# The first row slice of the modulation taken in two halves, with the first half's loads issued ahead

## The chip, the core and the metric

The kernel runs on one core of a Trainium2 chip. Five engines work from queues of their own, each in program order: TensorE (PE; its weight loads are shown apart as PEld), VectorE (DVE), ScalarE (ACT), GpSimd (POOL) and SyncE (SP), which here only issues the loads and stores (its DMA queue is SPq). They wait for each other through semaphores. The metric is the device time of one execution in microseconds (us); lower is better.

## The reference, cut to what matters

One layer of a hybrid block on 256 latent and 256 context tokens of width 2048, all in float32. Only the start of it is touched by the change: a modulation vector made from a conditioning vector, an RMSNorm scaled and shifted by it, and a projection of the result.

```python
sh_m, sc_m, ... = split(silu(c) @ w_ada + b_ada, 6)        # latent tokens
csh_m, csc_m, ... = split(silu(c_ctx) @ w_ada + b_ada, 6)  # context tokens
hc = rmsnorm(ctx, norm_mix_w) * (1 + csc_m) + csh_m
hl = rmsnorm(x, norm_mix_w) * (1 + sc_m) + sh_m
p = hl @ w_in          # w_in: 2048 x 13376, columns x | B | C | dt | z | pool | fourier | gates
# SSD, pooling and Fourier branches of p, gated sum, w_out, gated residual,
# then RMSNorm, SwiGLU (w_ffn_gate, w_ffn_up, w_ffn_down), gated residual, final RMSNorm
```

## The kernel before

**Stages.** All large products run as a list of stages. A stage has one weight load of 512 KB (256 rows of a weight as a tile `raw` of 128 x 2 x 512) and matmuls that use it. Each float32 weight is split in two parts by `split` (lines 123 to 125): ACT casts it to fp32r (`whi`, line 124), then DVE subtracts to get the rest (`wlo`, line 125). `mm3` (lines 130 to 133) makes one product from three matmuls of 128x512: hi by hi, hi by lo, lo by hi. `stream` walks through the list: for stage i it first issues loads up to stage i + lead + 4 (`load_upto`), then writes the splits of all stages up to i + lead (`split_upto`), then the stage's own matmuls. `lead` is 2. So the cast of a later stage's weight stands in ACT's queue, and its subtraction in DVE's queue, ahead of the work of the stage that is being written.

**The first sixteen stages.** The 2048 rows of the input are cut into eight slices j of 256 rows, that is two row tiles k of 128. For slice j, two stages run: `stage_b` multiplies the slice by 512 columns of `w_in` into four PSUM accumulators `b_acc`, kept over all slices; `stage_x0` multiplies it by another 512 columns, into PSUM tiles `aux` that are copied or added to `x_sum` in SBUF (line 391 on ACT for j = 0, line 394 on DVE after that). At its end it adds the slice to `dt_acc` with weights `dtp` (lines 400 and 401), which are split from the load `dtw` by `split_dt`; that is written after stage 0. There are four PSUM banks for `aux` tiles; `dt_acc` holds one for all of these stages.

**The modulation of a slice.** Before slice j can be multiplied, its rows of `xnT` (the normalised tokens, turned by PE's transposes of line 285) are modulated. Shift and scale come from 4 MB of `w_ada`, eight loads of 512 KB (`fetch`). `ada_tile` multiplies each by `stat` (line 314: matmuls with 32 columns of weights, four side by side); after the eighth, ACT copies the sums to SBUF (`adasb`, line 318) and `ada_sums` adds them up over partitions (line 324). `modulate` makes scale and shift on DVE (lines 335 to 337), applies them (line 344), casts the result on ACT (`hh`, line 345) and subtracts on DVE (`hl`, line 348). For slices 1 to 7 these pieces stand between the matmuls of the slice before. For slice 0 nothing stands beside them: all of slice 0's eight loads, matmuls and steps are written ahead of the first stage.

**Queues.** All loads go through SP's one queue in the order in which they are written: constants, the eight token tiles, slice 0's eight `w_ada` loads, three `w_in` loads (`load_upto(3)`), slice 1's eight `w_ada` loads, `dtw`, then the rest from `stream`. ACT, DVE and PE run what is written for them in that order and let nothing pass.

Of the kernel before, what the change touches and what calls it, by code (L numbers as in the profile page):

```python
# [11 lines left out]
F32 = mybir.dt.float32  # L12
# [4 lines left out]
P = 128  # L17
# [65 lines left out]
def hybrid_block(ctx: ExitStack, tc, io):  # L83
# [20 lines left out]
    def load(dst, src):  # L104
        nc.sync.dma_start(dst, src)
# [4 lines left out]
    def Q(shape, dt=F32, nme="q"):  # L110
        return qp.tile(shape, dt, tag="Q", name=nm(nme))
# [15 lines left out]
    def rows(w, k0, nk, c0, n):  # L127
        return w[k0 * P : (k0 + nk) * P, c0 : c0 + n].rearrange("(k p) n -> p k n", p=P)
# [191 lines left out]
    def ada_sums(j):  # L320
        if j >= 8:
            return
        for i in range(4):
            T.matmul(aps[j][:, 2 * i : 2 * i + 2], aps[j, "sb"][:, i * P : (i + 1) * P], SEL, start=True, stop=True)

    def modulate(j):
        if j >= 8:
            return
        k2 = slice(2 * j, 2 * j + 2)

        def col(o):
            return pp[:, o + 2 * j : o + 2 * j + 2].unsqueeze(2).to_broadcast([P, 2, 2])

        r = aps[j][:, 0:8].rearrange("p (a b) -> p a b", b=2)
        V.tensor_tensor(Sm[:, k2, :], r[:, 0:2], col(PP_BSHM), ALU.add)
        V.tensor_tensor(Am[:, k2, :], r[:, 2:4], col(PP_BSCM), ALU.add)
        V.scalar_tensor_tensor(Am[:, k2, :], Am[:, k2, :], 1.0, col(PP_NM), ALU.add, ALU.mult)
        hh[j] = H([P, 2, CH], F32R, nme="hh")
        hl[j] = H([P, 2, CH], F32R, nme="hl")
        for k in range(2):  # L340
            kt = 2 * j + k
            for s in range(2):
                v = xnT[j][:, k, s * 256 : (s + 1) * 256]
                V.tensor_scalar(v, v, Am[:, kt, s : s + 1], Sm[:, kt, s : s + 1], ALU.mult, ALU.add)
            S.copy(hh[j][:, k, :], xnT[j][:, k, :])
            yield
        for k in range(2):
            V.tensor_tensor(hl[j][:, k, :], xnT[j][:, k, :], hh[j][:, k, :].bitcast(F32), ALU.subtract)

    for i in range(8):  # L350
        fetch(0, i)
    scale_rows(0)
    for t in range(1, 4):
        scale_rows(t)
# [7 lines left out]
    dtp = []  # L362
    dt_acc = []

    def feature(ps, parts, j, o, first, last):

        hi, lo = parts
        for k in range(2):
            mm3(ps, hi[:, k, o : o + P], lo[:, k, o : o + P], hh[j][:, k, :], hl[j][:, k, :],
                first and k == 0, last and k == 1)  # L370

    def stage_b(j):
        def mm(parts):
            for ct in range(4):
                feature(b_acc[ct], parts, j, ct * P, j == 0, j == 7)
                for i in (2 * ct, 2 * ct + 1):
                    ada_tile(j + 1, i)
                    fetch(j + 2, i)
        return mm

    def stage_x0(j):
        def mm(parts):
            mod = modulate(j + 1)
            for ct in range(4):
                if ct:
# [3 lines left out]
                if j == 0:
                    x_sum[0, ct] = Q([P, 2, 256], nme="xin")  # L390
                    S.copy(x_sum[0, ct].rearrange("p a b -> p (a b)"), ps)
                else:
                    v = x_sum[0, ct].rearrange("p a b -> p (a b)")
                    V.tensor_tensor(v, v, ps, ALU.add)
                if ct == 0:
                    ada_sums(j + 1)
            for k in range(2):
                kt = 2 * j + k
                w = dtp[kt // 8][:, kt % 8, :]
                T.matmul(dt_acc[0], w, hh[j][:, k, :], start=kt == 0, stop=False)  # L400
                T.matmul(dt_acc[0], w, hl[j][:, k, :], start=False, stop=kt == KT - 1)
        return mm

    for j in range(8):
        add(rows(w_in, 2 * j, 2, B_OFF, CH), CH, stage_b(j), room=0)
        add(rows(w_in, 2 * j, 2, 0, CH), CH, stage_x0(j), room=0)

    b_acc.extend(acc() for _ in range(4))
    dt_acc.append(aux())
    load_upto(3)  # L410
    for i in range(8):
        fetch(1, i)
    dtw = H([P, KT, 64], nme="dtw")
    load(dtw, rows(w_in, 0, KT, DT_OFF, 64))
    for i in range(8):
        ada_tile(0, i)
    ada_sums(0)

    dtp.extend(H([P, 8, P], F32R, nme="dtp") for _ in range(2))
    for _ in modulate(0):  # L420
        pass

    def split_dt():
        for i in range(2):
            split(dtp[i][:, :, 0:64], dtp[i][:, :, 64:128], dtw[:, 8 * i : 8 * i + 8, :])
    stages[0].after.append(split_dt)

    bin_ = []

# [1053 lines left out]
    plan_ada(u_all[:32], s_u, s_q)  # L1483
    plan_ada(u_all[32:], s_q, s_o + 10)
    plan_ada(units_of(G_F), s_g + 2, s_d - 4)
    load_upto(6)
    split_upto(1)
    stream()
    for e in list(beside):
# [80 lines left out]
```

## Time and profile before

| | |
|---|---|
| median of three runs | 1902.11 us (1901.12 to 1902.36) |
| the profiled execution's own time | 1902.28 us |
| its span on the core | 1900.5 us |
| PE busy | 1845.0 us (97%) |
| DVE busy | 1247.2 us (66%) |
| ACT busy | 855.0 us (45%) |
| chain that ended last: PE, DMA, DVE, ACT | 81%, 7%, 5%, 4% |
| mean granted TensorE clock | 0.992 |

The span is the time from the first to the last record of the core; 1.8 us of the execution's own time lie around it. The page of the profile also cuts the span into 40 slices of 47.5 us and gives each engine's busy share in them. The chain that ended last is followed back from the last instruction: at each step to what released it, or to the instruction before it on its engine.

### The profile page before, as it was taken

To read this page: it belongs to the slowest core of one execution; us is meant where nothing else is said; L and a number is where in the kernel's file an instruction comes from. 1 tells how busy PE (TensorE), PEld (TensorE's weight loads), DVE (VectorE), ACT (ScalarE), POOL (GpSimd) and SP (SyncE) were. 2 spreads that over 40 slices of the span, in tenths; PEclk is the share of its full clock that TensorE was granted. 3 is DMA by queue.
4 is the path that set the end of the run, shared out by engine and by line. 5 is a ranking of instruction groups with operands and counts; after the bars stand their busy time and mean duration, and the time that the engine had idled before them with its cause. 6 is when DMAs were issued, how large, how long until landed. Compare 5 with 4: busy or idle time off the path is not lost.

```text
span 1900.5 us, 23216 instructions
## 1 busy us (share of the span) xinstructions
PE 1845.0 (97%) x8796; PEld 1483.7 (78%) x8796; DVE 1247.2 (66%) x1508; ACT 855.0 (45%) x1216; POOL 0.2 (0%) x4
## 2 busy tenths in 40 slices
PE   5999999999999999999999998999999999999997
PEld 3667887777777788887777777888888888888885
DVE  4445785778777587777888654777655555555567
ACT  4323445637456474533434346444443444434434
POOL 0000000000000000000000000000000000000000
PEclk9999999999999999999999999999999999999998
DMA  9992332556657456789989754888756666556653
GB/s 330 358 342 75 114 112 67 179 169 216 201 163 242 142 178 211 220 256 321 332 315 322 267 199 129 284 282 288 257 190 196 190 188 188 190 197 189 191 192 127
DMA packets 211904, 409.19 MB, mean 215 GB/s; under 512 B 14672, under 2 KB 47568, under 8 KB 211792
## 3 DMA queue, kind: packets, MB, share of 16 engines
q1 hardware_dynamic: 211792, 407.71, 67.1%
q8 instruction: 69, 1.13, 0.3%
q14 instruction: 43, 0.35, 0.1%
HBM read 405.56 MB, written 2.10 MB: 215 GB/s over the span
## 4 chain that ended last, share of the span: by engine, by line
PE 81%; DMA 7%; DVE 5%; ACT 4%; issue 2%; SPq 1%; DVEq 0%; ACTq 0%
PE acc L131 23%; PE acc L133 23%; PE acc L132 23%; DMA raw<-w_ssd_out 4%; ACT whi L124 2%; PE aux L314 2%; DVE wlo L125 1%; DMA raw<-w_in 1%; DVE adacc L461 1%; DMA raw<-w_out 1%; PE aux L131 1%; PE aux L132 1%; PE aux L133 1%; PE aux L683 1%; PE aux L759 1%
## 5 line engine op out<-in xcount | busy, mean ns | idle before, releaser
L125 DVE TENSOR_TENSOR wlo<-raw,whi 128x1024 fp32r<-128x1024 f32 x548 | 669.4, 1223 | 564.9 <-ACT whi L124 559.9
L124 ACT CAST whi<-raw 128x1024 fp32r<-128x1024 f32 x548 | 575.3, 1052 | 805.0 <-PE acc L133 613.5
L131 PE MATMUL acc<-whi,h2h 128*128 128x512 f32 x700 | 273.6, 391 | 4.4 <-ACT h2h L124 4.4
L133 PE MATMUL acc<-whi,h2l 128*128 128x512 f32 x700 | 273.1, 390 | 0.0
L132 PE MATMUL acc<-wlo,h2h 128*128 128x512 f32 x700 | 272.6, 389 | 0.0
L131 PE MATMUL acc<-whi,lh 128*128 128x512 f32 x640 | 256.7, 401 | 3.5 <-ACT gt L981 3.3
L132 PE MATMUL acc<-wlo,lh 128*128 128x512 f32 x640 | 250.5, 391 | 2.4 <-DVE wlo L125 2.4
L133 PE MATMUL acc<-whi,ll 128*128 128x512 f32 x640 | 249.7, 390 | 0.0
L131 PEld LDWEIGHTS acc<-whi,h2h 128*128 128x128 f32 x700 | 131.5, 188 | 31.8 <-ACT h2h L124 5.0
L461 DVE SCALAR_TENSOR_TENSOR adacc<-araw,sil,adacc 128x1024 f32<-128x1024 f32 x120 | 153.4, 1278 | 2.1 <-DMA araw<-w_ada 2.0
L133 PEld LDWEIGHTS acc<-whi,h2l 128*128 128x128 f32 x700 | 131.5, 188 | 28.3 <-DVE h2l L125 0.9
L132 PEld LDWEIGHTS acc<-wlo,h2h 128*128 128x128 f32 x700 | 131.6, 188 | 27.1
L132 PEld LDWEIGHTS acc<-wlo,lh 128*128 128x128 f32 x640 | 120.3, 188 | 31.5 <-DVE wlo L125 5.6
L131 PEld LDWEIGHTS acc<-whi,lh 128*128 128x128 f32 x640 | 120.2, 188 | 31.5 <-ACT gt L981 4.1
L133 PEld LDWEIGHTS acc<-whi,ll 128*128 128x128 f32 x640 | 120.1, 188 | 25.3
L131 PE MATMUL acc<-whi,ah 128*128 128x512 f32 x336 | 131.0, 390 | 0.0
L133 PE MATMUL acc<-whi,al 128*128 128x512 f32 x336 | 130.7, 389 | 0.0
L132 PE MATMUL acc<-wlo,ah 128*128 128x512 f32 x336 | 130.7, 389 | 0.0
L131 PE MATMUL acc<-hh,whi 128*128 128x512 f32 x256 | 104.9, 410 | 3.6 <-ACT whi L124 3.6
L132 PE MATMUL acc<-hl,whi 128*128 128x512 f32 x256 | 100.5, 393 | 0.0
L133 PE MATMUL acc<-hh,wlo 128*128 128x512 f32 x256 | 100.5, 392 | 0.0
L133 PEld LDWEIGHTS acc<-whi,al 128*128 128x128 f32 x336 | 63.1, 188 | 13.1
(291 smaller groups left out, 2272.6 us busy)
## 6 DMA issues: line engine op xcount, KB each, us to landing
raw<-w_in SPq DMA_DIRECT2D x208, 512.0 KB, 4.2
araw<-w_ada SPq DMA_DIRECT2D x128, 512.0 KB, 4.9
raw<-w_ffn_gate SPq DMA_DIRECT2D x88, 512.0 KB, 3.8
raw<-w_ffn_up SPq DMA_DIRECT2D x88, 512.0 KB, 3.8
raw<-w_ffn_down SPq DMA_DIRECT2D x88, 512.0 KB, 3.6
raw<-w_ada SPq DMA_DIRECT2D x64, 512.0 KB, 9.2
raw<-w_ssd_out SPq DMA_DIRECT2D x32, 512.0 KB, 6.1
raw<-w_out SPq DMA_DIRECT2D x32, 512.0 KB, 4.6
```

The costliest lines, as they stand in the source:

```text
L124: S.copy(hi, src)
L125: V.tensor_tensor(lo, src, hi.bitcast(F32), ALU.subtract)
L131: T.matmul(out, ah, bh, start=first, stop=False)
L132: T.matmul(out, ah, bl, start=False, stop=False)
L133: T.matmul(out, al, bh, start=False, stop=last)
L314: T.matmul(aps[j][32 * k : 32 * k + 32, o], stat[:, 4 * p + k, :], raws[j, i][:, k, :], start=p == 0, stop=p == 3)
L461: V.scalar_tensor_tensor(a, self.raw, sil[:, kt : kt + 1], a, ALU.mult, ALU.add)
L683: T.matmul(ps, btk[:, 2 + t, :], xc[d][t], start=t == 0, stop=t == 1)
L759: T.matmul(seg, m, rh, start=n == 0, stop=n == 3)
```

## The change

Slice 0 is taken as two halves h of one row tile (128 rows) each, in loads, modulation and products. `fetch_half` loads 8 x 128 x 128 of `w_ada`, four loads of 512 KB for a half, where `fetch` loads 4 x 128 x 256. The four loads of half 0, the `w_in` load of stage 0, the four loads of half 1, the `w_in` load of stage 1, `dtw` and the eight `w_ada` loads of slice 1 are issued in that order; the loads of stage 2 and beyond come from `stream`. Ahead of the first stage only half 0 is modulated. Stage 0 (`first_b`) multiplies half 0 by the `b` columns and then makes the `w_ada` sums of half 1. Stage 1 (`first_x`) multiplies half 0 by the `x` columns, modulates half 1 beside that, splits and uses `dtw`, and then does half 1 with both weights, with the `w_ada` sums and the modulation of slice 1 between. Stages 0 and 1 have `lead` 1 in place of 2. The product with the `x` columns goes to PSUM and to `x_sum` once for each half.

```diff
+    def fetch_half(h, i):
+        raws[0, h, i] = H([P, 8, P], nme="raw")
+        load(raws[0, h, i], rows(w_ada, 8 * (i % 2), 8, i // 2 * D + h * P, P))
+
+    def ada_half(h):
+        ps = aps[0, h] = aux([P, 2, P])
+        for i in range(4):
+            for k in range(8):
+                kt = 8 * (i % 2) + k
+                T.matmul(ps[32 * (k % 4) : 32 * (k % 4) + 32, i // 2, :], stat[:, kt, :], raws[0, h, i][:, k, :],
+                         start=kt < 4, stop=kt >= 12)
+        aps[0, h, "sb"] = Q([P, 2, P], nme="adasb")
+        S.copy(aps[0, h, "sb"], ps)
...
+    def modulate_half(h):
...
+        for s in range(2):
+            v = xnT[0][:, h, s * 256 : (s + 1) * 256]
+            V.tensor_scalar(v, v, Am[:, h, s : s + 1], Sm[:, h, s : s + 1], ALU.mult, ALU.add)
+        S.copy(hh[0][:, h, :], xnT[0][:, h, :])
+        V.tensor_tensor(hl[0][:, h, :], xnT[0][:, h, :], hh[0][:, h, :].bitcast(F32), ALU.subtract)
...
-    for i in range(8):
-        fetch(0, i)
+    for i in range(4):
+        fetch_half(0, i)
...
+    def first_b(parts):
+        parts0.append(parts)
+        for ct in range(4):
+            feature(b_acc[ct], parts, 0, ct * P, True, False, (0,))
+        ada_half(1)
+
+    def first_x(parts):
+        for ct in range(4):
+            ps = aux()
+            feature(ps, parts, 0, ct * P, True, True, (0,))
+            add_x(ct, ps, True)
+            if ct == 0:
+                sums_half(1)
+                modulate_half(1)
+        split_dt()
+        add_dt(0, 0)
+        for ct in range(4):
+            feature(b_acc[ct], parts0[0], 0, ct * P, False, False, (1,))
+            for i in (2 * ct, 2 * ct + 1):
+                ada_tile(1, i)
+                fetch(2, i)
+        mod = modulate(1)
+        for ct in range(4):
+            if ct:
+                next(mod, None)
+            ps = aux()
+            feature(ps, parts, 0, ct * P, True, True, (1,))
+            add_x(ct, ps, False)
+            if ct == 0:
+                ada_sums(1)
+        add_dt(0, 1)
...
+        if j == 0:
+            stages[0].lead = stages[1].lead = 1
...
-    load_upto(3)
-    for i in range(8):
-        fetch(1, i)
+    load_upto(1)
+    for i in range(4):
+        fetch_half(1, i)
+    load_upto(2)
     dtw = H([P, KT, 64], nme="dtw")
     load(dtw, rows(w_in, 0, KT, DT_OFF, 64))
     for i in range(8):
-        ada_tile(0, i)
-    ada_sums(0)
+        fetch(1, i)
+    ada_half(0)
+    sums_half(0)
...
-    load_upto(6)
     split_upto(1)
     stream()
```

**The load queue.** These are SP's rows from the last `w_ada` load of the first group on, of before. `raw` with `w_in` are the loads of stages 0, 1, 2 and, behind `dtw`, of stage 3.

```order
L105 DMA raw_142<-w_ada 128x4x256
L105 DMA raw_304<-w_in 128x2x512
L105 DMA raw_306<-w_in 128x2x512
L105 DMA raw_308<-w_in 128x2x512
L105 DMA raw_310<-w_ada 128x4x256
...
L105 DMA raw_324<-w_ada 128x4x256
L105 DMA dtw_326<-w_in 128x16x64
L105 DMA raw_394<-w_in 128x2x512
```

And of the change, where the three `w_in` loads are those of stages 0, 1 and 2:

```order
L105 DMA raw_134<-w_ada 128x8x128
L105 DMA raw_296<-w_in 128x2x512
L105 DMA raw_298<-w_ada 128x8x128
...
L105 DMA raw_304<-w_ada 128x8x128
L105 DMA raw_306<-w_in 128x2x512
L105 DMA dtw_308<-w_in 128x16x64
L105 DMA raw_310<-w_ada 128x4x256
...
L105 DMA raw_324<-w_ada 128x4x256
L105 DMA raw_390<-w_in 128x2x512
```

Stage 2's load, `raw_308` before, is `raw_390` now: it was the eleventh load behind the token tiles and is the twentieth now, behind the eight of slice 1.

**ACT in the first two stages.** Before, from the copy of slice 0's sums on (`whi` 400, 404, 408 and 493 are the casts for stages 0 to 3; `xin` are the copies to `x_sum`, `hh_513` belongs to slice 1):

```order
L318 COPY adasb_361<-aux_328 128x512
L345 CAST hh_372<-xnT_117 128x512 x2
L124 CAST whi_400<-raw_304 128x1024
L124 CAST whi_404<-raw_306 128x1024
L124 CAST whi_408<-raw_308 128x1024
L318 COPY adasb_483<-aux_418 128x512
L124 CAST dtp_367<-dtw_326 128x8x64
L124 CAST dtp_368<-dtw_326 128x8x64
L124 CAST whi_493<-raw_394 128x1024
L391 COPY xin_504<-aux_497 128x512
```

And of the change, from the copy of half 0's sums on:

```order
L338 COPY adasb_359<-aux_326 128x256
L358 CAST hh_368<-xnT_117 128x512
L124 CAST whi_386<-raw_296 128x1024
L124 CAST whi_396<-raw_306 128x1024
L338 COPY adasb_445<-aux_412 128x256
L124 CAST whi_449<-raw_390 128x1024
L410 COPY xin_457<-aux_453 128x512
L358 CAST hh_368<-xnT_117 128x512
L410 COPY xin_472<-aux_468 128x512
L410 COPY xin_478<-aux_474 128x512
L410 COPY xin_484<-aux_480 128x512
L124 CAST dtp_363<-dtw_308 128x8x64
```

Stage 2's cast (`whi_449`) now stands between the copy of half 1's sums and everything else of stage 1: the copies of the `x` products, half 1's `hh` and the two casts of `dtw`. On DVE its subtraction `wlo_450` stands in the same way ahead of the three small operations that begin half 1's modulation.

**PE in stage 1.** Of the change, from the last matmuls of half 1's sums on (`aux_453`, `468`, `474`, `480` are the four `x` products of half 0, `aux_295` is `dt_acc`, `acc_291` the first `b` accumulator):

```order
L335 MATMUL aux_412<-raw_304,stat_103 32x128 x8
L131 MATMUL aux_453<-hh_368,whi_396 128x512
...
L342 MATMUL aux_412<-cc_73,adasb_445 128x2 x2
L131 MATMUL aux_468<-hh_368,whi_396 128x512
...
L131 MATMUL aux_480<-hh_368,whi_396 128x512
L132 MATMUL aux_480<-hl_369,whi_396 128x512
L133 MATMUL aux_480<-hh_368,wlo_397 128x512
L418 MATMUL aux_295<-hh_368,dtp_363 128x512
L419 MATMUL aux_295<-hl_369,dtp_363 128x512
L131 MATMUL acc_291<-hh_368,whi_386 128x512
```

The last `x` product of half 0 (`aux_480`) takes the PSUM bank of the first (`aux_453`), which ACT's copy `xin_457` sets free. The `dt` matmuls (lines 418 and 419), which stood at the end of slice 0, now stand in its middle, ahead of all products of half 1 and of all `ada_tile` matmuls of slice 1. From the end of slice 1 on, the instructions of all engines stand as before, with the same waits.

More of the change, by code (lines that the diff above doesn't have):

```diff
@@ L324, in ada_sums, with sums_half, col @@
             T.matmul(aps[j][:, 2 * i : 2 * i + 2], aps[j, "sb"][:, i * P : (i + 1) * P], SEL, start=True, stop=True)
+    def fetch_half(h, i):
[10 more added lines that the diff above has]
+        S.copy(aps[0, h, "sb"], ps)
+    def sums_half(h):
+        for i in range(2):
+            T.matmul(aps[0, h][:, 0, 2 * i : 2 * i + 2], aps[0, h, "sb"][:, i, :], SEL, start=True, stop=True)
+    def modulate_half(h):
+        def col(o):
+            return pp[:, o + h : o + h + 1].to_broadcast([P, 2])
+        r = aps[0, h][:, 0, 0:4]
+        V.tensor_tensor(Am[:, h, :], r[:, 2:4], col(PP_BSCM), ALU.add)
+        V.tensor_tensor(Sm[:, h, :], r[:, 0:2], col(PP_BSHM), ALU.add)
+        V.scalar_tensor_tensor(Am[:, h, :], Am[:, h, :], 1.0, col(PP_NM), ALU.add, ALU.mult)
+        if h == 0:
+            hh[0] = H([P, 2, CH], F32R, nme="hh")
+            hl[0] = H([P, 2, CH], F32R, nme="hl")
+        for s in range(2):
[3 more added lines that the diff above has]
+        V.tensor_tensor(hl[0][:, h, :], xnT[0][:, h, :], hh[0][:, h, :].bitcast(F32), ALU.subtract)
     def modulate(j):
@@ L363, in hybrid_block, with feature, add_x, add_dt @@
     dt_acc = []
-    def feature(ps, parts, j, o, first, last):
+    def feature(ps, parts, j, o, first, last, ks=range(2)):
         hi, lo = parts
-        for k in range(2):
+        for k in ks:
             mm3(ps, hi[:, k, o : o + P], lo[:, k, o : o + P], hh[j][:, k, :], hl[j][:, k, :],
-                first and k == 0, last and k == 1)
+                first and k == ks[0], last and k == ks[-1])
+    def add_x(ct, ps, new):
+        if new:
+            x_sum[0, ct] = Q([P, 2, 256], nme="xin")
+            S.copy(x_sum[0, ct].rearrange("p a b -> p (a b)"), ps)
+        else:
+            v = x_sum[0, ct].rearrange("p a b -> p (a b)")
+            V.tensor_tensor(v, v, ps, ALU.add)
+    def add_dt(j, k):
+        kt = 2 * j + k
+        w = dtp[kt // 8][:, kt % 8, :]
+        T.matmul(dt_acc[0], w, hh[j][:, k, :], start=kt == 0, stop=False)
+        T.matmul(dt_acc[0], w, hl[j][:, k, :], start=False, stop=kt == KT - 1)
+    parts0 = []
+    def first_b(parts):
[28 more added lines that the diff above has]
+        add_dt(0, 1)
     def stage_b(j):
@@ L388, in mm @@
                 feature(ps, parts, j, ct * P, True, True)
[L389 to L394, printed above, removed]
+                add_x(ct, ps, False)
                 if ct == 0:
@@ L397, in mm @@
             for k in range(2):
[L398 to L401, printed above, removed]
+                add_dt(j, k)
         return mm
     for j in range(8):
-        add(rows(w_in, 2 * j, 2, B_OFF, CH), CH, stage_b(j), room=0)
-        add(rows(w_in, 2 * j, 2, 0, CH), CH, stage_x0(j), room=0)
+        add(rows(w_in, 2 * j, 2, B_OFF, CH), CH, stage_b(j) if j else first_b, room=0)
+        add(rows(w_in, 2 * j, 2, 0, CH), CH, stage_x0(j) if j else first_x, room=0)
+        if j == 0:
+            stages[0].lead = stages[1].lead = 1
     b_acc.extend(acc() for _ in range(4))
     dt_acc.append(aux())
-    load_upto(3)
-    for i in range(8):
-        fetch(1, i)
+    load_upto(1)
+    for i in range(4):
+        fetch_half(1, i)
+    load_upto(2)
     dtw = H([P, KT, 64], nme="dtw")
@@ L415, in hybrid_block @@
     for i in range(8):
-        ada_tile(0, i)
-    ada_sums(0)
+        fetch(1, i)
+    ada_half(0)
+    sums_half(0)
     dtp.extend(H([P, 8, P], F32R, nme="dtp") for _ in range(2))
-    for _ in modulate(0):
-        pass
+    modulate_half(0)
     def split_dt():
@@ L425, in split_dt @@
             split(dtp[i][:, :, 0:64], dtp[i][:, :, 64:128], dtw[:, 8 * i : 8 * i + 8, :])
-    stages[0].after.append(split_dt)
     bin_ = []
```

## The prediction

> **What bounds the kernel now.** The page comes first: span, PE's slices, the DMA engines' slices.
>
> ```profile
> span 1900.5 us, 23216 instructions
> ...
> PE   5999999999999999999999998999999999999997
> ...
> DMA  9992332556657456789989754888756666556653
> ```
>
> PE is the bound but in the first slice of 47.5 us, where it is half idle and the DMA engines are full. The change lies there. The chain of waits, in order of time (start us, us, what), shows how PE's unbroken work begins:
>
> ```profile
> 19.95 9.12 DMA raw<-w_ada
> 29.11 0.68 PE aux L314 x8
> 29.82 0.59 ACT adasb L318
> 30.46 1.07 PE aux L324 x8
> 32.08 0.75 DVE xnT L344 x2
> 32.91 1.21 ACT hh L345 x2
> 34.11 0.96 ACT whi L124
> 35.11 0.80 PE acc L131
> ```
>
> The eighth `w_ada` load lands at 29.05, the sums and the modulation take until 35.11, and only then does the first product run. PE's timeline gives the other fixed point:
>
> ```profile
> 54.65 0.39 PE L401 MATMUL aux<-hl,dtp 128*128 128x512 f32 x1
> 54.88 0.39 PE L131 MATMUL acc<-hh,whi 128*128 128x512 f32 x1
> ```
>
> Slice 1 begins at 54.88, with no gap of PE since 35.11. From slice 1's end on, instructions and waits are the same in both kernels. The chain over the whole span, by engine and by line:
>
> ```profile
> PE 81%; DMA 7%; DVE 5%; ACT 4%; issue 2%; SPq 1%; DVEq 0%; ACTq 0%
> PE acc L131 23%; PE acc L133 23%; PE acc L132 23%; DMA raw<-w_ssd_out 4%; ACT whi L124 2%; PE aux L314 2%; DVE wlo L125 1%; DMA raw<-w_in 1%; DVE adacc L461 1%; DMA raw<-w_out 1%; PE aux L131 1%; PE aux L132 1%; PE aux L133 1%; PE aux L683 1%; PE aux L759 1%
> ```
>
> is PE's for 81%; the 4% on `w_ssd_out` are loads into buffers that earlier stages free, so they come later when PE does. What the change moves at slice 1's start it moves at the end. I look for that time.
>
> **The load queue.** Two rows of the list of DMA issues (median us to landing, each for one load) with their starts in SP's timeline:
>
> ```profile
> 19.95 1.87 SPq L105 DMA_DIRECT2D raw<-w_ada  x1
> raw<-w_ada SPq DMA_DIRECT2D x1, 512.0 KB, 9.1
> 39.42 5.58 SPq L105 DMA_DIRECT2D raw<-w_in  x1
> raw<-w_in SPq DMA_DIRECT2D x1, 512.0 KB, 9.6
> ```
>
> The eighth load behind the token tiles lands at 19.95 + 9.1 = 29.05; stage 3's weight, the 21st, at 39.42 + 9.6 = 49.0. That is 13 loads, `dtw` among them, in 19.95 us: 1.535 us each. Nothing but this rate paces the queue there. In the change stage 2's weight (`raw_390`) is the 20th load, also with `dtw` ahead of it: it lands at R = 29.05 + 12 x 1.535 = 47.5 us, if the eight half loads take as long as the old ones. Their rows have 512 B where the old ones have 1 KB. The nearest rows, packets in 0.1 us with only `dtw` (256 B) and with only `w_ada` (1 KB) under way:
>
> ```profile
> DMA packets 82, 0.02 MB, mean 210 GB/s; under 512 B 82, under 2 KB 82, under 8 KB 82
> DMA packets 33, 0.03 MB, mean 338 GB/s; under 512 B 0, under 2 KB 33, under 8 KB 33
> ```
>
> So 1.2 ns and 3.0 ns a packet. A 512 B packet costs no more than a 1 KB packet and no less than one of 256 B. 1024 packets then take 1.25 to 3.1 us, against 1.55 by the second row: nothing lost, or at most 1.55 us a load and R = 59.9. On the line between both rows a packet takes 1.8 ns and a load 1.84 us, 0.3 more, R = 49.9. I take R = 48.5, between no loss and the line, since 1 KB and 2 KB loads run at one rate here, so that packets do not set it. The Trainium skill, DMA: Bandwidth & Descriptors, section Specifications, puts the smallest transfer at line rate at 512 B: by that R is 47.5 and the sum 1 us smaller; the 256 B row agrees that shorter ones are slow, and no row here shows 512 B.
>
> **The gain that the change is after.** PE's transposes end at 25.14, and half 0's four loads, the fourth behind the tokens at 29.05 - 4 x 1.5 = 23.0, no longer hold it:
>
> ```profile
> 24.05 1.09 PE L285 MATMUL aux<-cc,xt 128*128 128x128 f32 x8 [0.30 <-ACT xnT L291]
> 41.33 1.00 PE aux L314 x16
> 43.91 1.00 PE aux L314 x16
> 49.10 0.79 PE aux L324 x8
> ```
>
> Half 0's sums are 64 records as all of slice 0's were, with half the columns. By the second row a record takes 62 ns; with half the columns 31 to 62, so 2.0 to 4.0 us; I take 3.2. From the end of the sums to the first product were 35.11 - 29.79 = 5.3 us; half the columns in the copy (-0.25), half the sums over partitions (-0.5) and one cast less (-0.55) leave 4.0. The first product starts at 25.1 + 3.2 + 4.0 = 32.3, 2.8 us earlier. But half 1's sums, 3.2 us, now stand on PE's path; they were hidden behind loads. PE then does half 0's 12 `b` products (37.4 if the clock is low, as below), half 1's sums (40.6 to 41.4), and three `x` products with the partition sums, and stands at `aux_480` at about 44.
>
> **The stall.** `aux_480` needs ACT's copy `xin_457`, and that stands behind `whi_449`, which waits for `raw_390` until 48.5. What ACT and DVE then still have to do, by rows of the same operations in slice 0 before:
>
> ```profile
> 48.06 1.14 ACT L124 CAST dtp<-dtw 128x512 fp32r<-128x512 f32 x2
> 49.12 1.05 ACT L124 CAST whi<-raw 128x1024 fp32r<-128x1024 f32 x1
> 52.56 0.62 ACT L345 CAST hh<-xnT 128x512 fp32r<-128x512 f32 x1 [1.91 <-DVE xnT L344]
> 53.09 0.58 ACT L391 COPY xin<-aux 128x512 f32<-128x512 f32 x1
> 54.09 1.07 ACT L391 COPY xin<-aux 128x512 f32<-128x512 f32 x2
> 48.72 1.29 DVE L125 TENSOR_TENSOR dtp<-dtw,dtp 128x512 fp32r<-128x512 f32 x2 [10.13 <-ACT dtp L124]
> 50.19 1.23 DVE L125 TENSOR_TENSOR wlo<-raw,whi 128x1024 fp32r<-128x1024 f32 x1 [0.18 <-ACT whi L124]
> 51.34 0.15 DVE L335 TENSOR_TENSOR Sm<-aux,pp 128x4 f32<-128x4 f32 x1
> ```
>
> Step by step: the cast starts at R + 0.1; the subtraction 1.07 later (49.12 to 50.19), R + 1.1; the modulation 1.15 after that, R + 2.3; half 1's `hh` 1.22 later (51.34 to 52.56), R + 3.5; three `xin` copies at R + 4.0, 4.5 and 5.0 (each about 0.5); the `dtp` cast at R + 5.5; its subtraction 0.66 later, R + 6.1, done R + 6.8. PE gets `aux_480` done at about R + 2.5 and then waits at the `dt` matmul until **R + 6.9 = 55.4**. Behind that matmul PE has in order all of half 1 and all of slice 1's sums.
>
> **What is left of slice 0 then.** From 41.33 to 43.91 PE did 16 sums records (1.00) and six products (1.58). Three products after a change of tile shape take 0.9, others 0.23 each (54.65 to 54.88). So: `dt` 0.46; four times three products and 16 records, 4 x 1.9 - 0.2 = 7.4; the first `x` product 0.9; partition sums 0.8; the other nine 2.2; `dt` 0.46: **12.2 us**. Two additions. One is the clock, in columns behind PE, PEld, DVE, ACT and POOL busy: PEclk, DMA share, GB/s:
>
> ```profile
> 33.00:34.00 1.00, 0.00 (x0) 0.00 (x0) 0.90 (x3) 1.00 (x2) 0.00 (x0) 0.50 1.10 348
> 38.00:39.00 1.00, 1.00 (x10) 0.39 (x12) 0.59 (x1) 0.00 (x0) 0.00 (x0) 0.50 1.09 346
> 39.00:40.00 1.00, 1.00 (x17) 0.43 (x7) 0.00 (x0) 0.00 (x0) 0.00 (x0) 0.98 1.10 346
> ```
>
> Before, an idle time of 3.6 us brings the granted clock to 0.50, and it stays there until 39.0, 3.9 us into the products: 1.95 us lost. The two stalls here, 5 and 4.4 us, should do the same: **+1.9**. (The Trainium skill, TensorE: Matmul & The Clock Gate, Part 1, gives windows of some 3.4 us for both changes; that would be 1.7.) The other is slice 1's `hl`: its chain on DVE, before,
>
> ```profile
> 68.56 0.15 DVE L335 TENSOR_TENSOR Sm<-aux,pp 128x4 f32<-128x4 f32 x1
> 71.51 1.28 DVE L348 TENSOR_TENSOR hl<-xnT,hh 128x512 fp32r<-128x512 f32 x2
> ```
>
> takes 2.95 us to the start of `hl` and 0.65 more to its first half, covered by 18 products and `dt` after the partition sums; now only 9 products and half the `dt` stand there, 2.66 us. PE waits about **0.85**.
>
> **The sum.** Slice 1 begins at R + 6.9 + 12.2 + 1.9 + 0.85 = R + 21.85 = 70.35, against 54.88: 15.5 us later. The profiled execution took 1902.28 us with a span of 1900.5, 0.17 from the median of 1902.11; 1902.3 + 15.5 = **1917.8 us**. The gain of 2.8 us at the front is not in the sum: PE only reaches its stall earlier. Slice 0's early half, the extra 64 records and the shorter copies all end ahead of R and change nothing as long as they do (44 against 48.5, a margin of 4.5). Later work is the same and finds its loads earlier, never later.
>
> **Rivals.**
>
> *The early start carries through, not slower.* Place: ACT's queue between `adasb_445` and `dtp_363`. If the whole chain of 6.9 us were over when PE reaches the `dt` matmul at about 45, that is if `raw_390` landed before 38, only PE's own work would count: -2.8 for the start, +3.2 for half 1's sums, +0.4 for their second partition sums, +0.85: about 1904; with 2.0 for the sums and no low clock, 1900. For it: nothing that I see. Against it: it needs 20 loads in the time in which 13 or 14 land. Chance 0.04.
>
> *The load is in time, the queue is not.* If `raw_390` had landed when ACT gets to its cast, at about 42, the chain would still end at 48.9 and slice 1 would begin at 63.8, 8.9 later: 1911. It needs a rate 1.5 times that of the rows. Chance 0.03.
>
> *Half loads at a packet's price.* The 512 B loads are slow as a whole, with R between 50 and 59.9: 1919.5 to 1929. The 256 B row speaks against the far end, since the shorter packet is cheaper. Chance 0.06.
>
> That the change doesn't do what it says is ruled out by the order: half 0's loads are first in the queue.
>
> **How the numbers follow.** My case has 0.87. Its own ends: R = 47.5 without the clock's 1.9 and the 0.85 gives 66.6, 1914.0; R = 49.9 with all gives 71.75, 1919.2. The range reaches to the second rival and over the near part of the third, **1911 to 1923**; the far part and the first rival, under 0.1, are left out. About 0.2%, 3.8 us, is what a measurement of this kernel tells from no change. Faster by more would need the first rival and some 2 us beyond its best end: 0.01. Within: the rest of it, 0.04 with rounding. Slower: 0.95.
>
> **What would show it.** In the changed profile: the first product near 32.3, and the last of half 1's sums by 42; then PE idle until R, with `raw_390` landing at 47.5 to 50 and `whi_449` starting there; a second gap of 4 us of PE before line 418, released by DVE's `dtp`; a clock of 0.50 in both; slice 1's first product near 70. The forecast is wrong if `whi_449` starts by 43, if PE has no gap ahead of line 418, or if a time lost by slice 1's start is won back later, for which some later wait before must have been for a load that nothing of PE's paces.

## The result and the profile after

| | before | after |
|---|---|---|
| median | 1902.22 us (1901.12 to 1906.54, 5 runs) | 1920.47 us (1918.85 to 1923.38, 5 runs) |
| profiled execution, its span | 1902.28, 1900.5 us | 1919.34, 1917.6 us |
| mean granted clock | 0.992 | 0.988 |

The changed kernel is slower: the ratio is 1.0094, 95% interval 1.008 to 1.0109, so 15 to 21 us. The forecast was 1917.8 us, 15.5 above before.

The page of the changed kernel, its span, the slices of PE and of the DMA engines and the chain by engine and line:

```profile
span 1917.6 us, 23352 instructions
...
PE   4799999999999999999999898999999999999997
...
DMA  9993342466666546779999763888856666556653
...
PE 82%; DMA 6%; DVE 5%; ACT 5%; issue 1%; SPq 0%; DVEq 0%; ACTq 0%
PE acc L131 23%; PE acc L133 23%; PE acc L132 23%; DMA raw<-w_ssd_out 3%; ACT whi L124 2%; DVE wlo L125 2%; PE aux L314 1%; DMA raw<-w_in 1%; DVE adacc L538 1%; DMA araw<-w_ada 1%; PE aux L131 1%; PE aux L760 1%; PE aux L836 1%; PE aux L132 1%; PE aux L133 1%
```

PE's first slice falls from 5 to 4 tenths and the second from 9 to 7; the rest of the row is almost what it was, and the chain is still PE's, for 82% (81% before), with 3% on `w_ssd_out` (4%). The loss is in the first 75 us, and PE's timeline there shows it (start, duration, what; in brackets the idle time ahead of the row and what ended it):

```profile
31.51 0.50 PE L131 MATMUL acc<-hh,whi 128*128 128x512 f32 x1 [2.94 <-ACT whi L124]
...
36.57 1.95 PE L335 MATMUL aux<-raw,stat 128*32 128x128 f32 x64
...
53.92 0.79 PE L131 MATMUL aux<-hh,whi 128*128 128x512 f32 x1 [12.67 <-ACT xin L410]
...
59.17 0.77 PE L418 MATMUL aux<-hh,dtp 128*128 128x512 f32 x1 [3.61 <-DVE dtp L125]
...
73.18 0.39 PE L131 MATMUL acc<-hh,whi 128*128 128x512 f32 x1
74.52 0.50 PE L132 MATMUL acc<-hl,whi 128*128 128x512 f32 x1 [0.95 <-DVE hl L383]
```

The first product runs 3.6 us earlier than before (35.11). Then PE stands for 12.67 us ahead of the fourth `x` product and for 3.61 us ahead of the `dt` matmul. Slice 1 begins at 73.18 and waits for `hl` behind its first matmul, so it begins in effect at 74.3, 19.4 us later than before. ACT's timeline says what PE waited for:

```profile
38.59 0.37 ACT L338 COPY adasb<-aux 128x256 f32<-128x256 f32 x1 [1.34 <-PE aux L335]
52.34 1.04 ACT L124 CAST whi<-raw 128x1024 fp32r<-128x1024 f32 x1 [13.38 <-DMA raw<-w_in]
53.29 0.58 ACT L410 COPY xin<-aux 128x512 f32<-128x512 f32 x1
...
57.66 1.16 ACT L124 CAST dtp<-dtw 128x512 fp32r<-128x512 f32 x2
```

and SP's row of the load of stage 2's weight, then the list of DMA issues for this row alone (its last number is the time to landing), when it came:

```profile
43.71 1.37 SPq L105 DMA_DIRECT2D raw<-w_in  x1
```

```profile
raw<-w_in SPq DMA_DIRECT2D x1, 512.0 KB, 8.6
```

ACT is idle for 13.38 us with the `xin` copies in its queue, because the cast of stage 2's weight stands first and the weight lands at 43.71 + 8.6 = 52.3. That is the prediction's R.

### The profile page after: what moved, and what is told of

It reads as the page before. It is cut to its first block, busy times and chain, and to the rows that moved or that the text cites. A ratio compares the mean times of both kernels' runs of the same rounds, so it can differ in the third digit from the quotient of the medians.

```text
span 1917.6 us, 23352 instructions
## 1 busy us (share of the span) xinstructions
PE 1846.3 (96%) x8860; PEld 1486.4 (78%) x8860; DVE 1249.7 (65%) x1515; ACT 855.4 (45%) x1217; POOL 0.2 (0%) x4
## 4 chain that ended last, share of the span: by engine, by line
PE 82%; DMA 6%; DVE 5%; ACT 5%; issue 1%; SPq 0%; DVEq 0%; ACTq 0%
PE acc L131 23%; PE acc L133 23%; PE acc L132 23%; DMA raw<-w_ssd_out 3%; ACT whi L124 2%; DVE wlo L125 2%; PE aux L314 1%; DMA raw<-w_in 1%; DVE adacc L538 1%; DMA araw<-w_ada 1%; PE aux L131 1%; PE aux L760 1%; PE aux L836 1%; PE aux L132 1%; PE aux L133 1%
```

## How the runs are read

Three theories were set against each other. **Theory 1**: the queues of ACT and DVE stand behind stage 2's cast, so R sets slice 1's start. **Theory 2**: the halves cost PE the time themselves, whatever the order. **Theory 3**: the loads with 512 B rows cost it as such.

Two rows serve as marks in every run. The last eight transposes that PE makes tell how early the tokens were ready, before any `w_ada` load counts; the first addition to `x_sum` in slice 1 tells by how much the stretch of the change has moved the rest. The second mark, of before and of the changed kernel:

```profile
67.96 0.68 DVE L394 TENSOR_TENSOR xin<-xin,aux 128x512 f32<-128x512 f32 x1
87.50 0.68 DVE L413 TENSOR_TENSOR xin<-xin,aux 128x512 f32<-128x512 f32 x1
```

The first mark stands at 24.05 before (its row is in the prediction) and between 22.94 and 24.92 in the others. It differs between executions that issue the same token loads, so it is taken off:

| run | first mark, less 24.05 | second mark, less 67.96 | second less first | by the timed ratio (95% interval) |
|---|---|---|---|---|
| the change | +0.4 | +19.5 | +19.1 | +17.9 (15 to 21) |
| weight early (e1) | -0.7 | +6.2 | +6.9 | +9.1 (6.5 to 11.8) |
| cast later (e2) | -0.4 | +7.5 | +8.0 | +8.9 (5.9 to 11.8) |
| full loads (e3) | 0.0 | +18.2 | +18.2 | +17.9 (15 to 20) |
| before, half loads (e4) | -0.6 | +4.1 | +4.7 | +4.4 (2.7 to 6.3) |
| dt last (e5) | +0.3 | +16.1 | +15.9 | +15.6 (13 to 18) |
| before, 40 filling matmuls (e6) | +0.9 | +2.2 | +1.3 | +0.4 (-1.3 to 2.1) |
| weight early, dt last (e7) | +0.1 | +4.2 | +4.0 | +1.9 (0.2 to 3.6) |
| e7 and split later (e8) | +0.4 | +3.3 | +2.9 | +2.1 (0.4 to 3.8) |
| full loads, weight early (e9) | -1.1 | +7.2 | +8.3 | +9.7 (7.0 to 12.2) |
| before, 19 filling matmuls (e10) | +0.2 | +0.5 | +0.3 | -0.4 (-2.1 to 1.3) |
| slice 1's loads first (e11) | -0.5 | +4.6 | +5.1 | +6.9 (4.6 to 9.1) |
| e11 with filling (e12) | -0.7 | +4.8 | +5.5 | +5.3 (2.9 to 7.6) |

The last column is (ratio - 1) times the median of before on the same chip (1902.2 to 1904.3). In twelve of thirteen rows the stretch's shift lies within the interval of the time, and in e7 0.4 outside: as far as intervals of two to three us each way can tell, what is lost by slice 1 is lost at the end.

## What holds the queues: e1, e2, e5

**e1**, stage 2's weight issued behind `dtw`, ahead of slice 1's loads:

```diff
     load(dtw, rows(w_in, 0, KT, DT_OFF, 64))
+    load_upto(3)
     for i in range(8):
         fetch(1, i)
```

> The changed kernel, with stage 2's weight issued right behind dtw, ahead of slice 1's eight w_ada loads. Nothing else differs. Theory 1 (ACT's and DVE's queues stand behind stage 2's cast, so the landing R of its weight sets the dt matmul at R + 6.9 and slice 1 at R + 22): the weight takes the place of slice 1's first load and lands at about 39.4 in place of 52.3; ACT then reaches the cast at about 39.4 to 40, the chain ends near 47, slice 1 begins near 61.5 to 62 (in place of 74.3) and the time is some 12.5 us below the changed kernel's, 1907 to 1909 where the kernel before has 1902. Theory 2 (the two halves cost PE this time themselves, whatever the order of the loads): 1920 again. Theory 3 (the 512 B loads as such): 1920 again, as the loads up to slice 1's last are as slow as before.

Measured: 1911.73 us against 1904.31, ratio 1.0048 (1.0034 to 1.0062). ACT's cast of stage 2, and PE's rows with a gap:

```profile
38.05 1.05 ACT L124 CAST whi<-raw 128x1024 fp32r<-128x1024 f32 x1 [0.55 <-DMA raw<-w_in]
```

```profile
44.89 0.77 PE L418 MATMUL aux<-hh,dtp 128*128 128x512 f32 x1 [4.29 <-DVE dtp L125]
61.16 0.50 PE L132 MATMUL acc<-hl,whi 128*128 128x512 f32 x1 [0.95 <-DVE hl L383]
```

R goes from 52.3 to 38.05, the gap of 12.67 is gone, the `dt` matmul comes at R + 6.84 and slice 1 begins near 61.0, as theory 1 said. The time is higher than expected: 9.1 us above before's (6.5 to 11.8) where 5 to 7 were forecast, which lie only at the lower end of the interval. By the times about nine of the eighteen microseconds hang on R, by the marks twelve of nineteen; theories 2 and 3 had none of this.

**e2**, the same load order, but stage 2's cast and subtraction written behind stage 1's work:

```diff
-            stages[0].lead = stages[1].lead = 1
+            stages[0].lead, stages[1].lead = 1, 0
+            stages[1].first = lambda: load_upto(6)
```

> The changed kernel with its loads in the same order, but stage 2's cast and subtraction written behind stage 1's work in place of ahead of it. Theory 1 (the queues are held by that cast): R stays near 52, nothing waits for it any more before slice 1, PE has no gap of several us ahead of the fourth x product nor ahead of the dt matmul for the weight's sake; what ends last is then slice 1's own w_ada landing (50.9) plus its modulation, and slice 1 begins near 57.5: 1904 to 1907. Theory 2 (the halves cost PE the time themselves): 1920 again. Theory 3 (the 512 B loads): 1920 again, since no load moves.

Measured: 1912.40 us, ratio 1.0047 (1.0031 to 1.0062). PE's gaps:

```profile
43.66 0.50 PE L418 MATMUL aux<-hh,dtp 128*128 128x512 f32 x1 [2.63 <-DVE dtp L125]
59.26 0.50 PE L131 MATMUL acc<-hh,whi 128*128 128x512 f32 x1 [1.58 <-ACT whi L124]
61.19 0.73 PE L133 MATMUL acc<-hh,wlo 128*128 128x512 f32 x1 [1.20 <-DVE wlo L125]
```

No load was moved and no work taken away, and half of the loss goes: it is the place of the cast in the queue that costs. The time is 6 to 12 us above before's where 2 to 5 were expected, for the cast is now too late: slice 1 waits 1.58 us for it and 1.20 us for its subtraction.

**e5**, half 0's `dt` matmuls at the end of slice 0:

```diff
         split_dt()
-        add_dt(0, 0)
...
+        add_dt(0, 0)
         add_dt(0, 1)
```

> The changed kernel with half 0's two dt matmuls moved from ahead of half 1's products to the end of slice 0. Loads, casts and everything else stay. Theory 1 (slice 1 follows the chain that begins at R, the landing of stage 2's weight): R stays at 51.5 to 52.5; PE no longer waits for the dtp subtraction (R + 6.9) but only for half 1's cast, which ended at R + 4.0; slice 1 begins 2 to 3 us earlier than the 74.3 of the changed kernel, at 71.3 to 72.3 (a period of low clock more or less shifts this by up to 1.7), and the time is 2 to 3 us below it. If the dt matmul's place is not on the path: 74 again.

Measured: 1919.63 us against 1903.93, ratio 1.0082 (1.0068 to 1.0096). PE's rows:

```profile
56.03 0.79 PE L131 MATMUL acc<-hh,whi 128*128 128x512 f32 x1 [0.81 <-ACT hh L358]
71.11 0.50 PE L132 MATMUL acc<-hl,whi 128*128 128x512 f32 x1 [0.49 <-DVE hl L383]
```

The second gap shrinks from 3.61 to 0.81 us and slice 1 begins near 70.9 in place of 74.3. In the marks this is 3.2 us; the timed difference between the two ratios, 2.3 us, is smaller than their intervals, so the times alone could not tell it from nothing.

## Why R was 52.3 and not 48.5: e3, e4

**e3**, slice 0's weights in the eight loads of before, halves only in the work:

```diff
-    for i in range(4):
-        fetch_half(0, i)
+    for i in range(8):
+        fetch(0, i)
...
-    load_upto(1)
-    for i in range(4):
-        fetch_half(1, i)
     load_upto(2)
```

> The changed kernel, with slice 0's weights loaded by the eight loads of before (1 KB rows, all ahead of the first w_in load); only the sums, the modulation and the products go in halves. The early start is given up, the stall behind stage 2's weight stays. Theory 1 with the landing as the mis-sized term: R goes from 52.3 to the 47.5 worked out from the rate of before, slice 1 begins near 69.5, and the time is 4 to 5 us below the changed kernel's: 1915 to 1917. If the rate of the loads were the same for both row lengths: R stays near 52 and the time at 1920. Theory 2 (time of the halves on PE): 1920 or more, since PE now also starts later.

**e4**, the kernel before with slice 0's weights in eight loads with 512 B rows, all work as before:

```diff
-    for i in range(8):
-        fetch(0, i)
+    for h in range(2):
+        for i in range(4):
+            raws[0, h, i] = H([P, 8, P], nme="raw")
+            load(raws[0, h, i], rows(w_ada, 8 * (i % 2), 8, i // 2 * D + h * P, P))
```

> The kernel before, with slice 0's weights loaded as eight loads with 512 B rows in place of 1 KB rows; all sums, the modulation and the products as before. Theory: a load with 512 B rows takes 0.3 us more, as the packets' durations say (28 ns against half of 48 ns), so the eighth lands 2.4 us later and everything from the first product on moves by 2.4: 1904.6; up to 1907 if dips between the loads come on top (4.8 us were lost in the changed kernel to the 20th load). If the row length costs nothing: 1902.2, no change.

Measured: e3 1920.54 us, ratio 1.0094 (1.0081 to 1.0107), no better than the change; e4 1907.07 us, ratio 1.0023 (1.0014 to 1.0033). In e4, SP's rows of the first and of the eighth load, their times to landing from the list of DMA issues, and a window (behind the engines' busy times: PEclk, DMA share, GB/s):

```profile
7.40 0.38 SPq L105 DMA_DIRECT2D raw<-w_ada  x1
...
24.03 2.01 SPq L105 DMA_DIRECT2D raw<-w_ada  x1
```

```profile
raw<-w_ada SPq DMA_DIRECT2D x1, 512.0 KB, 11.5
...
raw<-w_ada SPq DMA_DIRECT2D x1, 512.0 KB, 7.5
```

```profile
26.00:28.00 2.00, 0.94 (x40) 0.68 (x30) 0.00 (x0) 0.00 (x0) 0.00 (x0) 1.00 1.21 293
```

The same window and the first load in the kernel before (its eighth is in the prediction):

```profile
26.00:28.00 2.00, 2.00 (x44) 1.09 (x36) 0.00 (x0) 0.00 (x0) 0.00 (x0) 1.00 1.09 358
```

```profile
7.96 0.38 SPq L105 DMA_DIRECT2D raw<-w_ada  x1
```

```profile
raw<-w_ada SPq DMA_DIRECT2D x1, 512.0 KB, 10.6
```

In e4 seven loads take 31.53 - 18.90 = 12.63 us, 1.80 us each; before they took 29.05 - 18.56 = 10.49, 1.50 each. In these windows the engines move 293 GB/s with 512 B rows where 1 KB rows go at 358. So eight half loads cost 2.4 us here, and the prediction had taken 1.0. (The price is not one number: in the changed kernel's own trace the first half load lands at 7.59 + 12.3 = 19.9 and the fourth at 17.98 + 6.7 = 24.7, 1.60 us apart.) At the second mark e4 stands 4.1 us behind before; 2.5 of it are the later landing of the eighth load. The rest is clock: it is granted at 0.50 from 30.0 to 43.6, in before from 32.2 to 39.0, so that the sums and the first products run slower.

e3 has none of the half loads, and yet its stage 2 weight does not land at 47.5. Its issue, its time to landing, a window, and slice 1's second product on PE:

```profile
40.73 1.38 SPq L105 DMA_DIRECT2D raw<-w_in  x1
```

```profile
raw<-w_in SPq DMA_DIRECT2D x1, 512.0 KB, 9.1
```

```profile
32.00:34.00 2.00, 0.00 (x0) 0.00 (x0) 1.26 (x4) 1.31 (x2) 0.00 (x0) 0.58 0.30 69
```

```profile
73.18 0.50 PE L132 MATMUL acc<-hl,whi 128*128 128x512 f32 x1 [0.93 <-DVE hl L384]
```

The weight lands at 49.8, 2.3 us late. Of this, 0.8 us were lost ahead of all these loads: the last token tile landed at 6.37 + 11.4 = 17.8, in before at 6.11 + 10.9 = 17.0. And between 32 and 34 us the DMA engines were nearly idle (share 0.30, 69 GB/s). This is the stretch just ahead of `dtw`'s landing at 35.6. The rate that the prediction took from before has a dip of that kind in it (200 GB/s from 44 to 46 us), but it is deeper here; what makes it deeper was not found out. And e3's slice 1 begins at R + 23.1 where the change has R + 22.0. The clock makes this difference. These windows run from the `dt` matmul to the end of the low clock, in the change and in e3:

```profile
59.17:62.92 3.75, 3.75 (x21) 2.06 (x21) 0.46 (x1) 0.00 (x0) 0.00 (x0) 0.50 1.10 348
56.70:63.03 6.33, 6.33 (x32) 3.14 (x36) 0.46 (x1) 0.00 (x0) 0.00 (x0) 0.50 1.10 349
```

The low clock ends at the same time in both, so e3, whose `dt` matmul comes earlier, has 2.6 us more of it, which cost half, 1.3 us. In e1 it lasts 5.9 us behind the `dt` matmul, and its slice 1 begins at R + 22.9. So e3 gains 2.5 us at R, gives back 1.1, and the times do not tell it from the change. Of theory 3 there remain some 2 us by which the short rows delay R.

## What is left without the stall: e7, e8, e9

**e7**, e1 and e5 together:

> The run with stage 2's weight ahead of slice 1's loads, plus the dt matmuls at the end of slice 0: both parts of the stall's chain taken off PE's path. Theory 1: half 1's first product starts when its cast is done, near 42.0 in place of the dt matmul at 44.9; slice 1 begins 2.9 us earlier than the 61.0 of that run, near 58, so some 3 us later than before: 1905 to 1908 by a before of 1902 to 1904. Theory 2 (the halves cost PE's time themselves) has nothing left to fall by: it would stay at 61.

**e8**, e7 with stage 2's split written behind half 1's modulation and `split_dt`:

```diff
+            stages[0].lead, stages[1].lead = 1, 0
+            stages[1].first = lambda: load_upto(6)
...
         split_dt()
+        split_upto(3)
```

> The run before this one, and stage 2's cast and subtraction written behind half 1's modulation and the split of dtw in place of ahead of them: no step of half 1 stands behind stage 2's weight any more. Theory 1 says that PE then runs from its first product (30.4) through slice 0 with hardly a gap, and that the next bound is slice 1's own w_ada: its last load lands at 50.8 (27 loads, eight of them with 512 B rows), and by the rows of the runs so far its sums and modulation take 1.0 and 5.6 us to the first product with hl. So slice 1 begins at 56.5 to 57.5, still 1.5 to 2.5 us later than before, although PE started 4.7 us earlier: 1904 to 1907. If instead the early start of PE is worth what it looks like (4.7 us less 2.4 for half 1's own sums), slice 1 begins near 53: 1900 to 1902, faster than before.

Measured: e7 1906.57 us, ratio 1.0010 (1.0001 to 1.0019); e8 1906.31 us, ratio 1.0011 (1.0002 to 1.0020). PE in e7:

```profile
58.86 0.50 PE L132 MATMUL acc<-hl,whi 128*128 128x512 f32 x1 [0.50 <-DVE hl L383]
```

and in e8, with two windows of the granted clock behind it:

```profile
51.28 0.64 PE L314 MATMUL aux<-raw,stat 128*32 128x256 f32 x8 [0.86 <-DMA raw<-w_ada]
58.17 0.39 PE L131 MATMUL acc<-hh,whi 128*128 128x512 f32 x1
```

```profile
50.30:53.70 3.40, 2.54 (x24) 1.72 (x21) 0.69 (x1) 0.59 (x1) 0.00 (x0) 1.00 1.05 383
53.70:57.10 3.40, 3.40 (x9) 2.62 (x10) 3.15 (x10) 1.28 (x3) 0.00 (x0) 0.50 1.10 351
```

In both, all but some 2 us of the loss is gone by the times (3 to 4 by the marks), so theory 2 falls: nothing of the halves' work was taken away. In e8 PE has no long gap up to slice 1's sums, where it waits for slice 1's last load: it lands at 51.25, and slice 1 begins 6.9 us later at 58.17. PE began 3.7 us earlier than before (31.42 against 35.11) and comes to slice 1 3.3 us later. Slice 1 came 0.7 us later than expected; a period of low clock from 53.7 to 57.1, 1.7 us, had not been reckoned with.

**e9**, e3 with stage 2's weight early, asks what PE's early start is worth once the weight is in time:

> The run with slice 0's weights in the eight full loads, and stage 2's weight issued behind dtw, ahead of slice 1's loads. Against the run that has half loads and the early weight (slice 1 at 61.0) it shows what the early start of PE is worth once the weight is in time: first product at 34.3 in place of 30.4. By the rows of that run the dt matmul follows 7.8 us behind the copy of half 1's sums, which stands here near 41.7: dt at 49.5, slice 1 some 16 us later, at 65 to 66, 4 to 5 us behind the run with half loads: a time 10 to 11 us above before's, 1913 to 1915. If the early start is worth nothing in any order: slice 1 near 61 and some 6 us above before.

Measured: 1913.54 us against 1903.56, ratio 1.0051 (1.0037 to 1.0064). The time is where it was expected, the trace is not: this execution's tokens came 1.1 us early (first mark), the chain from the copy of half 1's sums took 7 and not 7.8 us, and slice 1 began at 62.0 in place of 65. By the marks the early start is worth 8.3 - 6.9 = 1.4 us, against 4 to 5 expected; e9 has only 3.4 us of low clock behind its `dt` matmul where e1 has 5.9, which hides 1.3 us more. By the ratios of e1 and e9, which are the same within their intervals, it cannot be told from nothing.

## The clock: e6, e10

Both add matmuls without use to the kernel before (32 x 512 results from `stat` and `xnT[7]` into `b_acc`, which is begun anew later), so that PE isn't idle ahead of the first product: e6 40 of them, e10 19. The edit of e10:

```diff
     for i in range(8):
         ada_tile(0, i)
+        if i == 6:
+            idle(3)
+    idle(2)
     ada_sums(0)
+    idle(14)
```

> The kernel before, plus 40 matmuls without use (32 x 512 results into the b accumulators, which are begun anew later): 4 after each of slice 0's w_ada tiles 3 to 7, 20 between the partition sums and the first product. Nothing waits for them; they only keep PE busy while it waited for loads and for the modulation. The clock term (1.9 us in the prediction's sum) by itself: if the low granted clock from 32 to 39 comes from PE's idle time, it stays at 1.00, the products of 35 to 39 run at full speed, slice 1 begins 1.7 to 2 us earlier than the 54.88 of before, near 53, and the time is some 2 us (0.1%) below before's. If the low clock has another cause: 54.9 again, or later by what the added matmuls hold up.

> The kernel before with 19 added matmuls in place of 40 (one took 0.215 us in the run with 40, where they held the first product up by 2.6 us): 3 behind the seventh w_ada tile, 2 ahead of the partition sums (0.43 of the 0.70 us that PE waits there), 14 behind them (3.0 of the 3.60 us). Nothing waits for them now. If the idle time alone makes the low clock: the clock stays at 1.00 from 30 to 40, the first product still starts 6.1 us after the landing of the eighth load (29.05 to 35.11 before), slice 1 begins 17.8 us after it in place of 19.8, and the time is some 2 us, 0.1%, below before's. If the clock falls all the same, for PE's load in this stretch is too small: no change.

Measured: e6 1904.09 us, ratio 1.0002 (0.9993 to 1.0011); e10 1903.38 us, ratio 0.9998 (0.9989 to 1.0007). PE in e6 (two records for each of these matmuls), then the granted clock of e6 from 28 us to slice 1, and PE in e10:

```profile
34.81 4.50 PE L417 MATMUL acc<-xnT,stat 128*32 128x512 f32 x40
39.24 0.50 PE L131 MATMUL acc<-hh,whi 128*128 128x512 f32 x1
...
57.08 0.39 PE L131 MATMUL acc<-hh,whi 128*128 128x512 f32 x1
```

```profile
28.00:57.10 29.10, 29.10 (x245) 16.31 (x238) 12.17 (x25) 10.05 (x16) 0.00 (x0) 1.00 1.04 332
```

```profile
35.93 0.50 PE L131 MATMUL acc<-hh,whi 128*128 128x512 f32 x1
37.19 0.50 PE L133 MATMUL acc<-hh,wlo 128*128 128x512 f32 x1 [0.53 <-DVE wlo L125]
54.53 0.39 PE L131 MATMUL acc<-hh,whi 128*128 128x512 f32 x1
65.05 0.64 PE L314 MATMUL aux<-raw,stat 128*32 128x256 f32 x8 [0.65 <-DMA raw<-w_ada]
```

With PE kept busy the clock stays at 1.00, in e10 too. In e6 slice 0 takes 57.08 - 39.24 = 17.84 us from the first product to slice 1, against 54.88 - 35.11 = 19.77 before: 1.93 us is the low clock's price, and the prediction's term was 1.9. But 40 were too many: 20 in a row took 4.5 us and held the first product up. In e10 the first product comes 6.2 us behind the eighth load, as before, and slice 0 takes 18.6 us, since a wait of 0.53 us for `wlo` appears that the slow clock had hidden; in slice 1 another 0.65 us goes to a wait for slice 2's loads. Nothing is left that the times could show.

## The order that the runs point to: e11, e12

**e11** takes slice 1's loads ahead of stage 2's weight and of `dtw`, puts stage 2's split between slice 1's sums and its modulation, and the `dt` matmuls of slice 0 at the end of slice 1:

```diff
     load_upto(2)
-    dtw = H([P, KT, 64], nme="dtw")
-    load(dtw, rows(w_in, 0, KT, DT_OFF, 64))
     for i in range(8):
         fetch(1, i)
+    load_upto(3)
+    dtw = H([P, KT, 64], nme="dtw")
+    load(dtw, rows(w_in, 0, KT, DT_OFF, 64))
...
-        split_dt()
-        add_dt(0, 0)
...
+        split_upto(3)
         mod = modulate(1)
...
-        add_dt(0, 1)
...
+    stages[2].after.append(split_dt)
```

> The changed kernel in the order that the runs point to: slice 1's eight w_ada loads ahead of stage 2's weight and of dtw; stage 2's cast and subtraction written between slice 1's w_ada sums and its modulation; dtw's split behind stage 2 and half 0's and half 1's dt matmuls at the end of slice 1. Nothing of slice 0 stands behind a late load then, and slice 1's last w_ada load lands two places, 3.1 us, earlier than the 51.25 of the run with the split moved: near 48.1. With 6.6 to 6.9 us for its sums, modulation and hl, slice 1 begins at 54.7 to 55.5, where before's began at 54.88, with 0.9 us of dt matmuls put off into slice 1: a tie or up to 2 us above before's, 1903 to 1906. If the early start of PE were worth more than the loads let through, 1900 or less.

**e12** adds 13 filling matmuls behind half 0's partition sums.

> The run before this one, with 13 matmuls without use between half 0's partition sums and the first product (2.8 of the 2.95 us in which PE waited there), so that the granted clock does not fall. If slice 1 hangs on its loads, as theory 1 now has it, PE only gets to its wait for them 2 us sooner, and the time is that of the run without them, within 1 us. If slice 1 hangs on PE's work, slice 1 begins some 2 us earlier, near 53, and the time is 1 to 2 us below before's: 1901 to 1903.

Measured: e11 1908.89 us, ratio 1.0036 (1.0024 to 1.0048); e12 1908.22 us, ratio 1.0028 (1.0015 to 1.0040). PE in e11 at slice 1's second product, then in e12 from slice 1's first product on, and e12's clock:

```profile
57.04 0.67 PE L132 MATMUL acc<-hl,whi 128*128 128x512 f32 x1 [1.25 <-DVE hl L383]
```

```profile
52.96 0.49 PE L131 MATMUL acc<-hh,whi 128*128 128x512 f32 x1 [0.83 <-ACT hh L380]
54.71 0.50 PE L132 MATMUL acc<-hl,whi 128*128 128x512 f32 x1 [1.25 <-DVE hl L383]
...
56.84 1.08 PE L314 MATMUL aux<-raw,stat 128*32 128x256 f32 x8 [0.69 <-DMA raw<-w_ada]
```

```profile
53.20:56.60 3.40, 1.69 (x6) 0.86 (x5) 3.40 (x6) 2.52 (x3) 0.00 (x0) 0.99 1.08 361
56.60:63.40 6.80, 6.22 (x34) 2.85 (x38) 1.52 (x2) 0.00 (x0) 0.00 (x0) 0.50 1.10 349
```

In e12 slice 1 begins in effect at 54.5, 0.4 us earlier than before's, and 2.3 us earlier than in e11, where its second product stands at 57.04. So it was PE's work, with the steps that follow slice 1's sums, and not slice 1's loads that ended last there, the second case of what was expected of e12; the time of that case, 1901 to 1903, was missed. The gain is gone within slice 1: its partition sums start at 70.40, before's at 66.61. The wait for `hl` (1.25 us) and the start of the first wait for slice 2's loads lie in the 3.4 us ahead of a low clock from 56.6 to 63.4, which costs some 3 us; the two waits for slice 2's loads, 0.69 and 0.34 us, cost one more. e11 missed too: the split ahead of the modulation holds slice 1's `hh` and `hl` up (0.85 and 1.25 us of waits), and a low clock from 57.2 to 60.6 follows. No version was found that beats the kernel before.

## Why the prediction was right, point by point

- **The mechanism held.** Stage 2's cast starts at R + 0.0 (52.34; forecast R + 0.1), PE has its two gaps, ended by `xin` and by `dtp`, the `dt` matmul comes at R + 6.9 (59.17 - 52.3; forecast the same), and slice 1 begins at R + 22.0 (forecast R + 21.85). e1 and e2 show that the queue behind the cast is the cause: either its load or its place, changed alone, takes half of the loss away, and e7 and e8 all but some 2 us.
- **The term that was mis-sized is R**: 52.3 measured, 48.5 taken, and the extreme of the likely range was 49.9. Of the 3.8 us, 1.2 were lost ahead of these loads: the last token tile landed at 6.28 + 11.9 = 18.2, in before at 17.0. The eight loads with 512 B rows cost 2.1 (R of the change less R of e3, net of the start) to 2.4 us (e4) where 1.0 was taken; the upper end of the range, interpolated between the 256 B and the 1 KB packets, was right. The rest, 1.5 us, appears with full loads too (e3) and goes with dips of the load rate. Runs with the same loads in the same order are near: R is 51.6 in e2 and 51.9 in e5.
- **The reason for taking 48.5 was misread.** The prediction went below the interpolated 49.9 because loads with 1 KB and with 2 KB rows ran at one rate. They did not quite: in before the eighth `w_ada` load lands at 29.05 and the third `w_in` load behind it at 24.08 + 9.2 = 33.3, 1.4 us each with 2 KB rows, against 1.50 with 1 KB.
- **The price of 512 B rows.** The Trainium skill, DMA: Bandwidth & Descriptors, section Specifications, has 512 B as the smallest transfer at line rate. The rows of e4 differ, 293 GB/s against 358 with 1 KB, and the measurement decides: what the prediction made of that rule, R = 47.5, was the farther end.
- **Smaller terms.** Half 0's sums took 1.95 us, not 3.2; the first product came at 31.51, not at 32.3. Both lie ahead of the stall and change nothing, as was said. The low clock's 1.9 us is 1.93 in e6, and the same in the change (3.75 us at 0.50 behind the `dt` matmul); that it came out so well is in part luck, for the same term is 3.2 in e3 and 3.0 in e1. Slice 1's `hl` wait is 0.95 where 0.85 was forecast.
- **From slice 1 to the end.** The step held within what the times resolve (the table above). In the profiled execution 19.4 us at slice 1 had become 17.1 at the end, which the prediction named as a sign of being wrong. Taken matmul by matmul from the end, the shift stays at 19.4 to 19.5 us up to 864 us of before, falls to 17.1 by 1100, and stays. Most other runs change in about the same stretch, 750 to 1220 us, and both ways (e2 from 7.5 to 10.5, e8 from 3.4 to 0.7). So it looks like scatter of single executions and not like recovery; what makes it was not looked into.
- **The rivals, and some luck.** The main case, given 0.87, ended at R = 49.9 and 1919.2 us; the measured R and time lie outside it, near the low end of the half loads at a packet's price, which had 0.06, though 2.7 of the 4.8 us by which R passed 47.5 are not the packets'. At slice 1 the sum was 3.9 us short, at the end 2.4 by the ratio: the time fell within the range because the range reached into that rival, and because single executions scatter by about as much. The early start does not carry through even with the stall gone: in e8 slice 1's loads end last, and in e12 waits and the low clock they come with take it back.

## What to carry to other kernels

A prefetched cast or copy in an in-order queue belongs behind every step that does not need it, for as long as its load is not sure to have landed: count the loads ahead of it, at the rate of their own row length, before it is put in front of work that feeds the bound engine. An earlier start of the first piece pays only as far as the loads of the pieces behind it come earlier too; where the queue is full, smaller pieces move the wait, and shorter rows make the loads dearer. Single traces begin up to 2 us apart (the first mark); a mark on a row ahead of the change, taken off, removes that part of the scatter.

## What was not expected of the hardware

Loads of 512 KB with 512 B rows landed 1.80 us apart in e4 (293 GB/s in the window shown) and 1.60 in the changed kernel, with 1 KB rows 1.50 (358 GB/s), with 2 KB rows 1.4. The granted clock changes in steps of about 3.4 us, and a full idle step isn't needed for it to fall: in e8 it went to 0.50 after a step in which PE was busy for 2.54 of 3.40 us (with a wait of 0.86 us and partition sums of two columns in it), in e12 after one with 1.69 of 3.40. The Trainium skill, TensorE: Matmul & The Clock Gate, Part 1, has such free-running windows of 3.4 us, and the steps here agree; it has the fall after an idle window, and these two rows show it after windows that were three quarters and half busy.
